# A decoder block with stick-breaking attention: where three parts of its first stage run, and how many buffers its modulation weights have

## The chip, the cores and the metric

The kernel runs on one core of a Trainium2 chip. The core has five engines, each with its own instruction queue: TensorE (matmuls; the profile shows PE, and PEld for its weight loads), VectorE (DVE), ScalarE (ACT), GpSimd (POOL) and SyncE (SP, which here only issues DMAs). Data lies in SBUF (128 partitions), matmul results in PSUM (eight banks of 128 x 512 float32). The metric is the device time of one execution in microseconds (us); lower is better.

## The reference

One layer, batch 1, 1024 tokens, width 1024, all float32. Cut to what matters:

```python
mod = jax.nn.silu(c) @ w_ada + b_ada
shift, scale, gate = jnp.split(mod, 3, axis=-1)
h = rms_norm(x, norm_gain) * (1.0 + scale[:, None, :]) + shift[:, None, :]
proj = h @ w_in                                   # 1024 x 8192
q, k, v, z_a, u, z_b, m_a, m_b = jnp.split(proj, offs, axis=-1)

attn = stick_breaking_attention(q, k, v)          # 16 heads of 64, causal
p_a = (attn * jax.nn.silu(z_a)) @ w_branch_a
pooled = multiscale_causal_pool(u, pool_w, pool_scale)
p_b = (pooled * jax.nn.silu(z_b)) @ w_branch_b
merged = jax.nn.sigmoid(m_a) * p_a + jax.nn.sigmoid(m_b) * p_b
x = x + gate[:, None, :] * (merged @ w_out)
return rms_norm(x, final_gain)
```

The change touches the first three lines and the first columns of `h @ w_in`.

## The kernel before

All large products are done in three matmuls. A float32 operand is split into a high part (a copy rounded to the type `F32R`, the profile's fp32r) and a low part (the operand minus the high part); high x high, high x low and low x high are added up in PSUM. So every weight tile and every block of h costs a copy, mostly on ScalarE, and a subtraction on VectorE or GpSimd.

The stages follow one another: (1) modulation, normalization and transposition of x, h, and the projection to u; (2) the rest of u, then v; (3) pooling, its gate and its branch; (4) attention, between whose steps the matmuls of the other projections are placed; (5) the two output products. The change acts on stage 1, the code under `with pool("init")`, lines 190 to 327. There 1024 is cut into KB = 8 blocks of P = 128.

**The modulation** of block kb needs shift and scale for 128 columns, that is 256 sums over the 1024 elements of silu(c). `load_mod(kb)` (L221) brings the 1 MB weight tile `wa` (128 partitions x 8 x 256) in; the tag "wa" has three buffers, and x4/x5 and x6/x7 later use the same tag. `modulation(kb)` (L227) multiplies the eight slices of 128 x 256 by a scalar per partition (`sc`) and adds them up in `acc` on VectorE: one `tensor_scalar_mul` (L232) and seven `scalar_tensor_tensor` (L234). Two matmuls with a column of ones (L237) then sum over the partitions into the PSUM tile `mps`, which has one bank; two ScalarE instructions make `mod` of it.

**x and h.** `norm_x` (L211) scales a block of 128 tokens: ScalarE sums the squares, GpSimd makes the factor (`st`), VectorE multiplies (L217). `turn_x` (L248) transposes four 128 x 128 blocks on TensorE into the PSUM tile `xt`, of which only one bank is left in this stage. `make_h` (L255) makes the transposed h of a block for 512 tokens: ScalarE applies `mod` (`hf`), ScalarE copies the high part, and the engine that is handed in subtracts for the low part (L260). In the loop over kb it is handed GpSimd (L307), for the second 512 tokens VectorE (L327).

**The first weights.** `first_w(i)` (L265) loads the weight tile of u's column block i (512 KB, two buffers "raw"), copies the high part on ScalarE and subtracts the low part on GpSimd (L271).

**The order.** The loop at L282 runs over kb = 0 to 8. TensorE's instructions, ScalarE's marked ones and the loads of SyncE are pinned to program order (`order`, `load`); VectorE's and GpSimd's instructions are placed by a scheduler at build time, which keeps each queue in a fixed order. A step kb holds a list `todo` of pairs (i, k): column block i of u against block k of h. Column block kb - 1 is new and catches up on all its k, the older ones take k = kb - 1 only; there are six such column blocks (NA) with a PSUM bank each. On TensorE a step is: the high-weight and low-weight matmul of the first pair with the high part of h, the modulation's matmuls, the same two matmuls of the other pairs, one matmul of each pair with the low part of h, and the transposes of block kb + 1. `busy(n)` (L241) adds matmuls whose result is not used, n each at the places that `BUSY` gives; the profile shows them as `ua<-ident,ones` and `ua<-wa,ones`. The SyncE queue takes the loads of wu and wa in turn, and each waits until its buffer is free.

After the loop come column blocks 6 and 7 of u, the second half of x and h, and the next pools.

Of the kernel before, what the change touches and what calls it, by code (L numbers as in the profile page):

```python
# [9 lines left out]
F32 = mybir.dt.float32  # L10
# [5 lines left out]
P = 128  # L16
D = 1024
S = 1024
KB = D // P
# [18 lines left out]
LO_V = (1, 1, 1, 1, 1, 1, 1, 0)  # L38
LO_PB = (1, 1, 1, 1, 1, 1, 2, 2)
HD = 64  # L40
BUSY = (6, 3, 3, 3, 6, 2, 0, 2)
EPS = 1e-6
WINDOWS = (2, 4, 8, 16)
# [5 lines left out]
def block_kernel(ctx, tc, a, out):  # L49
    nc = tc.nc  # L50
    v, act, gp = nc.vector, nc.scalar, nc.gpsimd
# [10 lines left out]
    def bank(tag, name):  # L62
        return psp.tile([P, 512], F32, tag=tag, bufs=BANKS[tag], name=name)
# [3 lines left out]
    g_d = dram.tile([1, D], F32, name="g_d")  # L67
    v_d = dram.tile([NP, P, 8, 4 * HD], F32, name="v_d")
    sb_d = dram.tile([KB, P, S], F32, name="sb_d")
# [6 lines left out]
    ones = const.tile([P, P], F32, name="ones")  # L76
# [11 lines left out]
    def order(op):  # L88
        def issue(*args, **kw):
            ins = op(*args, **kw)  # L90
            if pinned[0]:
                tc.keep_in_program_order(ins)
        return issue

    mm = order(nc.tensor.matmul)
# [94 lines left out]
    with pool("init") as init:  # L190
        sig = const.tile([P, 8], F32, name="csig")
        act.activation(sig, c_v, AF.Sigmoid)
        sc = const.tile([P, 8], F32, name="csilu")
# [8 lines left out]
        def load(dst, src):  # L202
            tc.keep_in_program_order(nc.sync.dma_start(dst, src))

        def load_x(sb):
            if sb in (4, 6):
                pr = init.tile([P, 2, D], F32, tag="wa", bufs=3, name=f"x{sb}")
                xs.extend([pr[:, 0], pr[:, 1]])
            load(xs[sb], a["x"][sb * P:(sb + 1) * P, :])

# [8 lines left out]
        was = {}  # L219

        def load_mod(kb, parts=1):  # L221
            was[kb] = init.tile([P, KB, 2 * P], F32, tag="wa", bufs=3, name=f"wa{kb}")
            n = KB // parts
            for i in range(parts):
                load(was[kb][:, i * n:i * n + n].rearrange("p k c -> p (k c)"), a["w_mod"][kb][:, i * n * 2 * P:(i + 1) * n * 2 * P])

        def modulation(kb):  # L227
            if kb == KB:
                return
            wa = was.pop(kb)  # L230
            acc = init.tile([P, 2 * P], F32, tag="acc", bufs=2, name=f"acc{kb}")
            v.tensor_scalar_mul(acc, wa[:, 0], sc[:, 0:1])  # L232
            for k in range(1, KB):
                v.scalar_tensor_tensor(acc, wa[:, k], sc[:, k:k + 1], acc, ALU.mult, ALU.add)  # L234
            mps = bank("av", f"mps{kb}")
            for i in range(2):
                mm(mps[:, i:i + 1], acc[:, i * P:(i + 1) * P], ones[:, 0:1], start=True, stop=True)  # L237
            order(act.activation)(mod[kb][:, 0:1], mps[:, 0:1], AF.Identity, bias=bada_v[:, kb:kb + 1])
            order(act.activation)(mod[kb][:, 1:2], mps[:, 1:2], AF.Identity, bias=affb[:, kb:kb + 1], scale=gain_v[:, kb:kb + 1])

        def busy(n, mov=ident):  # L241

            for _ in range(n):
                mm(accs[NA - 1][:, :P], ones, mov, start=True, stop=True)
# [3 lines left out]
        def turn_x(sh, kb):  # L248
            pt = xts[sh, kb] = bank("tr", f"xt{sh}_{kb}")
            for i in range(4):  # L250
                transpose(pt[:, i * P:(i + 1) * P], xs[4 * sh + i][:, kb * P:(kb + 1) * P])
                if (sh, kb) == (0, 0) and i < 3:
                    busy(BUSY[1 + i])

        def make_h(sh, kb, lo_eng):  # L255
            hf = init.tile([P, 512], F32, tag="hf", bufs=3, name=f"hf{sh}_{kb}")
            order(act.activation)(hf, xts.pop((sh, kb)), AF.Identity, bias=mod[kb][:, 0:1], scale=mod[kb][:, 1:2])
            sl = slice(sh * 512, sh * 512 + 512)
            order(act.copy)(h_hi[:, kb, sl], hf)
            lo_eng.tensor_sub(h_lo[:, kb, sl], hf, h_hi[:, kb, sl].bitcast(F32))  # L260
# [4 lines left out]
        def first_w(i):  # L265
            raw = wts.tile([P, KB, P], F32, tag="raw", bufs=2, name=f"wu{i}_raw")
            load(raw.rearrange("p k c -> p (k c)"), a["w_in"][CU + i])
            pl, tag, n = (first, "whl0", NA) if i < NA else (wts, "whl", 2)
            hl = pl.tile([P, 2, KB, P], F32R, tag=tag, bufs=n, name=f"wu{i}")
            order(act.copy)(hl[:, 0], raw)  # L270
            gp.tensor_sub(hl[:, 1], raw, hl[:, 0].bitcast(F32))  # L271
            return hl[:, 0], hl[:, 1]

        use = [copy_out(first, 3, u_d[i], f"u{i}") for i in range(KB)]
        load_mod(0, 2)
        for sb in range(4):
            load_x(sb)
            norm_x(sb)
# [3 lines left out]
        for kb in range(KB + 1):  # L282

            kp, sl = kb - 1, slice(0, 512)
            for kind in ("wm" if kb == 0 else "mw"):
                if kind == "m" and kb + 1 < KB:
                    load_mod(kb + 1)
                if kind == "w" and kb < NA:
                    whl.append(first_w(kb))
            todo = [(i, k) for i in range(min(kb, NA)) for k in range(0 if i == kp else kp, kb)]  # L290
            for n, (i, k) in enumerate(todo):
                if n == 1:
                    modulation(kb)
                    if kb == 2:
                        busy(BUSY[6])
                mm(accs[i], whl[i][0][:, k], h_hi[:, k, sl], start=k == 0, stop=False)
                mm(accs[i], whl[i][1][:, k], h_hi[:, k, sl], start=False, stop=False)
            if len(todo) < 2:
                if kb < 2:
                    busy(BUSY[4 * kb], was[0][:, 0, :P] if kb == 0 else ident)  # L300
                modulation(kb)
            for i, k in todo:
                mm(accs[i], whl[i][0][:, k], h_lo[:, k, sl], start=False, stop=k == KB - 1)
            if kb < KB:
                if kb == 0:
                    turn_x(0, 0)
                make_h(0, kb, gp)  # L307
                if kb + 1 < KB:
                    turn_x(0, kb + 1)
                if kb < 2:  # L310
                    busy(BUSY[5 + 2 * kb])
        pinned[0] = False
        for i in range(NA, KB):
            whl.append(first_w(i))
        for sb in range(4, 8):
            load_x(sb)
# [13 lines left out]
    with pool("vp") as vp:  # L330
# [11 lines left out]
        for hf in range(2):  # L342
            if hf == 0:
                wv.append([load_wv(1, k2) for k2 in range(4)])
            for sb in range(8):
                ss = slice(sb * P, (sb + 1) * P)
                ps = bank("pj", f"v{sb}_{hf}")
                for kb in range(KB):
                    hh, hl = h_hi[:, kb, ss], h_lo[:, kb, ss]
# [3 lines left out]

                vo = vp.tile([P, 8, 2, HD], F32R, tag="vo", bufs=3, name=f"vo{sb}_{hf}")
                pv = ps.rearrange("p (h d) -> p h d", d=HD)
                act.copy(vo[:, :, 0], pv)
# [84 lines left out]
    with pool("at") as at:  # L441
# [7 lines left out]
        def pair_tiles(p, use):  # L449

            def tile_(tag, shape, dt=F32R):
                return at.tile([P] + shape, dt, tag=tag, bufs=2, name=f"{tag}_{p}")
# [5 lines left out]
            elif use is use_za:  # L458
                pair[p].update(vv=tile_("vv", [8, 2, 2, HD]), za=tile_("za", [S], F32))

# [224 lines left out]
    with pool("fin") as fin:  # L685
# [29 lines left out]
        for sh in range(2):  # L715
# [24 lines left out]
            for i in range(4):  # L740
                sb = 4 * sh + i
# [86 lines left out]
```

## Time and profile before

| | |
|---|---|
| three runs | 1291.13, 1292.53, 1293.98 us |
| median | 1292.53 us |
| profiled execution | 1294.87 us |
| its span, first to last instruction | 1293.2 us |
| mean granted TensorE clock | 0.990 |
| TensorE busy, whole span | 1241.9 us (96%) |
| VectorE, ScalarE, GpSimd busy | 804.1, 548.1, 279.3 us |
| HBM read and written | 136.86 and 50.34 MB |

How to read the rows. All times are of the one profiled execution, in us unless ns is written. A row of the timeline or of the chain has the start, the duration, the engine, the line of the code, the operation, and the tiles as out<-in; x4 means that four instructions are merged in one row. L90 is the helper `order`, through which all matmuls go, so there the tile tells what it is. A plain float32 matmul leaves two records each for weight load and product. A row of the stretches (A:B) has the stretch's length, then busy time and count of PE, PEld, DVE, ACT and POOL, the granted clock (1.00 is full speed), the mean busy share of the DMA engines, and GB/s. A row by form has the shapes and the count, then total busy time in us and mean ns of one, then the idle time before them and what ended it. A row of waits has the total in us, the number of times and the longest.

### The profile page before, as it was taken

How to read it: one execution, taken by the hardware profiler on the slowest of the kernel's cores; microseconds unless marked ns; L12 is line 12 of the kernel's file. 1: busy time of each engine (PE TensorE's matmuls, PEld its weight loads, DVE VectorE, ACT ScalarE, POOL GpSimd, SP SyncE). 2: the span in 40 equal slices, each digit the busy share in tenths (PEclk: the TensorE clock that was granted, in tenths of full speed). 3: DMA queues.
4: the chain of work that ended last, by engine and by line, in shares of the span. 5: the costliest groups of instructions: out<-in, count | busy, mean ns of one | idle time of the engine just before them, and what ended most of it. 6: DMA issues, size and time to landing. Idle time of an engine off the chain costs nothing.

```text
span 1293.2 us, 16723 instructions
## 1 busy us (share of the span) xinstructions
PE 1241.9 (96%) x6094; PEld 1035.6 (80%) x6094; DVE 804.1 (62%) x1020; ACT 548.1 (42%) x1029; POOL 279.3 (22%) x397
## 2 busy tenths in 40 slices
PE   6799999989999999999999999999999998889997
PEld 5688888768888888888888888888888887667886
DVE  7915342899611177785877768686776743657654
ACT  4445331231101255565656556565655543312101
POOL 4610000102122332322313122231212211400001
PEclk9899999999999999999999999999999999899999
DMA  8528995862343411233323223232322237855512
GB/s 317 204 98 310 330 343 188 303 225 83 113 146 130 155 42 53 70 114 107 122 77 101 80 98 119 90 122 89 99 72 96 96 107 266 288 186 172 183 65 94
DMA packets 72804, 192.48 MB, mean 149 GB/s; under 512 B 7697, under 2 KB 21009, under 8 KB 70802
## 3 DMA queue, kind: packets, MB, share of 16 engines
q1 hardware_dynamic: 63106, 174.38, 39.4%
q10 hardware_dynamic: 9616, 17.04, 3.9%
q8 instruction: 48, 0.79, 0.2%
q14 instruction: 34, 0.28, 0.1%
HBM read 136.86 MB, written 50.34 MB: 145 GB/s over the span
## 4 chain that ended last, share of the span: by engine, by line
PE 78%; DVE 10%; issue 5%; DMA 4%; ACT 1%; POOL 1%; SPq 0%; POOLq 0%; DVEq 0%; ACTq 0%
PE p L90 30%; PE pb L90 7%; PE v L90 7%; PE avs L90 5%; PE o L90 5%; PE wzb L90 5%; PE z L90 5%; PE wt L90 4%; PE u L90 4%; PE pa L90 4%; DVE acc L234 2%; PE ua L90 1%; PE pool L90 1%; DMA wor<-in_w_out 1%; DVE om L557 1%
## 5 line engine op out<-in xcount | busy, mean ns | idle before, releaser
L90 PE MATMUL p<-hT,w 128*128 128x512 f32 x1920 | 538.2, 401 | 0.0
L90 PEld LDWEIGHTS p<-hT,w 128*128 128x128 f32 x1920 | 335.3, 189 | 45.9 <-issue 0.5
L557 DVE TENSOR_TENSOR_SCAN om<-om 128x512 f32<-128x512 f32 (+7 forms) x128 | 175.7, 1372 | 65.7 <-POOL om L555 41.1
L577 DVE TENSOR_TENSOR wt<-wt,wt 128x512 fp32r<-128x512 f32 (+1 forms) x160 | 101.1, 633 | 66.7 <-ACT wt L576 65.4
L550 ACT ACTIVATE om<-z 128x512 f32<-128x512 f32 (+2 forms) x192 | 94.3, 491 | 112.4 <-PE z L90 109.9
L555 POOL TENSOR_SCALAR_AFFINE_SELECT om<-om 128x128 f32<-128x128 f32 x128 | 62.0, 484 | 354.8 <-ACT om L550 318.1
L576 ACT CAST wt<-wt 128x512 fp32r<-128x512 f32 (+1 forms) x160 | 87.2, 545 | 74.9 <-PE wt L90 71.0
L90 PEld LDWEIGHTS avs<-wt,vv 128*128 128x128 f32 x640 | 96.0, 188 | 18.6 <-DVE tp L603 6.7
L558 DVE TENSOR_TENSOR be<-be,om 128x511 f32<-128x511 f32 (+7 forms) x128 | 102.4, 800 | 11.0
L90 PE MATMUL pa<-ga,wa 128*128 128x512 f32 x384 | 94.6, 402 | 10.9 <-DVE ga L698 3.9
L90 PE MATMUL avs<-wt,vv 128*128 128x256 f32 (+1 forms) x640 | 99.8, 278 | 4.5 <-DVE tp L603 4.5
L90 PEld LDWEIGHTS pa<-ga,wa 128*128 128x128 f32 x384 | 73.4, 194 | 31.0 <-DVE ga L698 5.2
L551 ACT ACTIVATE be<-z 128x512 f32<-128x512 f32 (+2 forms) x192 | 93.5, 487 | 0.0
L90 PE MATMUL wzb<-hT,wzb 128*128 128x512 f32 x384 | 92.2, 396 | 0.0
L90 PE MATMUL o<-wo,mhl 128*128 128x512 f32 (+1 forms) x408 | 89.6, 377 | 2.5 <-DVE mhl L114 2.5
L90 PEld LDWEIGHTS wt<-ident,be 128*128 128x128 f32 x576 | 72.4, 141 | 23.6 <-DVE wt L577 1.7
L90 PE MATMUL wt<-ident,be 128*128 128x128 f32 x576 | 89.1, 272 | 0.8 <-DVE wt L577 0.8
L90 PE MATMUL pb<-gb,wb 128*128 128x512 f32 x384 | 88.1, 391 | 0.0
L90 PE MATMUL v<-wv,hT 128*128 128x512 f32 x384 | 87.2, 389 | 0.0
L90 PEld LDWEIGHTS o<-wo,mhl 128*128 128x128 f32 x408 | 73.3, 188 | 17.3 <-DVE mhl L114 3.3
L90 PEld LDWEIGHTS wzb<-hT,wzb 128*128 128x128 f32 x384 | 73.1, 191 | 16.3 <-DVE zs L400 0.3
L90 PEld LDWEIGHTS pb<-gb,wb 128*128 128x128 f32 x384 | 72.1, 188 | 15.8
(118 smaller groups left out, 1538.9 us busy)
## 6 DMA issues: line engine op xcount, KB each, us to landing
w_raw<-in_w_in SPq DMA_DIRECT2D x40, 512.0 KB, 4.4
l_raw<-in_w_in SPq DMA_DIRECT2D x32, 512.0 KB, 5.5
wl_d<-l_raw SPq DMA_DIRECT2D x32, 512.0 KB, 5.0
w<-wl_d SPq DMA_DIRECT2D x32, 512.0 KB, 3.7
v_d<-vo SPq DMA_DIRECT2D x16, 512.0 KB, 5.3
vv<-v_d SPq DMA_DIRECT2D x8, 1024.0 KB, 5.7
wa_raw<-in_w_branch_a SPq DMA_DIRECT2D x16, 512.0 KB, 4.5
wa<-in_w_mod SPq DMA_DIRECT2D x7, 1024.0 KB, 5.5
```

What stands on the lines that cost most here:

```text
L90: ins = op(*args, **kw)
L234: v.scalar_tensor_tensor(acc, wa[:, k], sc[:, k:k + 1], acc, ALU.mult, ALU.add)
L550: act.activation(om[:, b0:b0 + n], zp[:, :n], AF.Sigmoid, scale=-0.125)
L551: act.activation(be[:, b0:b0 + n], zp[:, :n], AF.Sigmoid, scale=0.125)
L555: gp.affine_select(out=tl[:, :P], in_=tl[:, :P], pattern=[[1, P]], compare_op=ALU.is_gt, fill=fill, base=0, channel_multiplier=-1)
L557: v.tensor_tensor_scan(om[:, :W], om[:, :W], om[:, :W], 1.0, ALU.mult, ALU.min)
L558: v.tensor_mul(be[:, 1:W], be[:, 1:W], om[:, :W - 1])
L576: act.copy(wt[:, 0, :off], pt[:, :off])
L577: v.tensor_sub(wt[:, 1, :off], pt[:, :off], wt[:, 0, :off].bitcast(F32))
```

## The change

```diff
+KM = 6
...
         def load_x(sb):
             if sb in (4, 6):
-                pr = init.tile([P, 2, D], F32, tag="wa", bufs=3, name=f"x{sb}")
+                pr = init.tile([P, 2, D], F32, tag="wa", bufs=5, name=f"x{sb}")
...
         def load_mod(kb, parts=1):
-            was[kb] = init.tile([P, KB, 2 * P], F32, tag="wa", bufs=3, name=f"wa{kb}")
+            was[kb] = init.tile([P, KB, 2 * P], F32, tag="wa", bufs=5, name=f"wa{kb}")
...
             v.tensor_scalar_mul(acc, wa[:, 0], sc[:, 0:1])
-            for k in range(1, KB):
+            for k in range(1, KM):
                 v.scalar_tensor_tensor(acc, wa[:, k], sc[:, k:k + 1], acc, ALU.mult, ALU.add)
             mps = bank("av", f"mps{kb}")
             for i in range(2):
-                mm(mps[:, i:i + 1], acc[:, i * P:(i + 1) * P], ones[:, 0:1], start=True, stop=True)
+                for k in range(KM, KB):
+                    mm(mps[:, i:i + 1], wa[:, k, i * P:(i + 1) * P], sc[:, k:k + 1], start=k == KM, stop=False)
+                mm(mps[:, i:i + 1], acc[:, i * P:(i + 1) * P], ones[:, 0:1], start=False, stop=True)
...
             order(act.copy)(hl[:, 0], raw)
-            gp.tensor_sub(hl[:, 1], raw, hl[:, 0].bitcast(F32))
+            v.tensor_sub(hl[:, 1], raw, hl[:, 0].bitcast(F32))
...
                     turn_x(0, 0)
-                make_h(0, kb, gp)
+                make_h(0, kb, v)
```

`acc` now holds the sum of six slices. The other two go through TensorE: wa's slice is the weight, silu(c)'s column the moving operand, and the result is added to the same PSUM column as the sum of acc. For each half i the two new matmuls stand ahead of the one with acc, so with i = 1 they stand behind acc's product for i = 0. The low parts of the first weights (`first_w`, all eight column blocks of u) and of h's first 512 tokens are subtracted on VectorE instead of GpSimd. The tag "wa" has five buffers of 8 KB per partition instead of three.

## The prediction

> **What bounds the kernel now.** First the chain of work that ended last, on the page, then the busy time of the engines in stretches.
>
> ```profile
> span 1293.2 us, 16723 instructions
> ...
> PE 78%; DVE 10%; issue 5%; DMA 4%; ACT 1%; POOL 1%; SPq 0%; POOLq 0%; DVEq 0%; ACTq 0%
> ```
> ```profile
> 0.00:60.42 60.42, 41.80 (x180) 35.32 (x180) 50.56 (x63) 26.36 (x44) 33.59 (x31) 0.92 0.69 261
> 60.42:79.82 19.40, 19.40 (x88) 16.05 (x89) 8.15 (x13) 9.76 (x19) 5.97 (x9) 0.91 0.28 110
> 79.82:224.55 144.73, 144.51 (x650) 119.55 (x649) 52.86 (x54) 55.18 (x73) 5.26 (x18) 1.00 0.77 276
> ```
>
> TensorE carries most of the chain. It is idle 18.6 us (60.42 - 41.80) in the first 60.42 us, and 0.22 us in the 164 us after them. So a change that acts only in the first stage can pay only ahead of 60.42, and what it saves there reaches the end if the later work just starts earlier. The chain in order of time says what holds that stage (start, duration, what):
>
> ```profile
> 42.36 2.46 DVE acc L232
> ...
> 57.90 2.47 DVE acc L234
> ...
> 60.42 0.61 PE mps L90 x4
> 61.02 8.79 PE ua L90 x31
> 69.81 0.44 PE xt L90 x4
> ...
> 70.71 0.34 PE mps L90 x4
> 71.05 3.78 PE ua L90 x16
> ...
> 79.82 10.92 PE u L90 x48
> ```
>
> Up to 60.42 the chain is VectorE's accumulation of the modulation; from there TensorE runs through. The last wait is that for the sum of block 6 (the seventh mps); the eighth, at 70.71, is late for nobody. Some accumulation steps last 2.46 us, others do not. The timeline, with GpSimd's instructions beside VectorE's:
>
> ```profile
> 42.12 2.54 POOL L271 TENSOR_TENSOR wu<-wu_raw,wu 128x1024 fp32r<-128x1024 f32 x1
> ...
> 51.85 8.51 DVE L234 SCALAR_TENSOR_TENSOR acc<-wa,csilu,acc 128x256 f32<-128x256 f32 x7
> ...
> 53.58 1.48 POOL L260 TENSOR_TENSOR hT<-hf,hT 128x512 fp32r<-128x512 f32 x1 [1.92 <-ACT hT L90]
> 55.02 5.06 POOL L271 TENSOR_TENSOR wu<-wu_raw,wu 128x1024 fp32r<-128x1024 f32 x2
> ...
> 60.28 0.34 DVE L232 TENSOR_SCALAR acc<-wa,csilu 128x256 f32<-128x256 f32 x1
> ...
> 60.66 3.61 DVE L234 SCALAR_TENSOR_TENSOR acc<-wa,csilu,acc 128x256 f32<-128x256 f32 x7
> ```
>
> A free step takes 0.34 us (L232) or 3.61/7 = 0.516 us (L234). The long one at 42.36 starts inside GpSimd's subtraction of 42.12 and ends 0.16 us after it; the row of 51.85 takes 8.51 us for seven steps, beside GpSimd rows of 1.48 and 5.06 us. VectorE stands still while GpSimd subtracts. By form, over the first 80 us:
>
> ```profile
> L234 DVE SCALAR_TENSOR_TENSOR acc<-wa,csilu,acc 128x256 f32<-128x256 f32 x56 | 40.4, 726 | 1.8
> L271 POOL TENSOR_TENSOR wu<-wu_raw,wu 128x1024 fp32r<-128x1024 f32 x8 | 20.1, 2518 | 0.0
> L260 POOL TENSOR_TENSOR hT<-hf,hT 128x512 fp32r<-128x512 f32 x8 | 10.9, 1357 | 21.5 <-ACT hT L90 21.5
> L232 DVE TENSOR_SCALAR acc<-wa,csilu 128x256 f32<-128x256 f32 x8 | 9.1, 1137 | 2.9 <-DMA wa<-in_w_mod 2.9
> ```
>
> Against the free steps the stall is 56 x (0.726 - 0.516) + 8 x (1.137 - 0.34) = 18.1 us, nearly all ahead of 60.42.
>
> **The change part by part.** *Two of the eight blocks to TensorE.* VectorE loses 2 x 0.516 = 1.03 us for each of the eight sums; one now costs 0.34 + 5 x 0.516 = 2.92 us. TensorE gains four matmuls for each, of one column with full 128x128 weights. The two matmuls of before appear as four records, so four more are eight records. No such product with wa as weights stands in the trace. Nearest rows: four mps records take 0.34 us on the chain where nothing is waited for (0.085 each); four transposes 0.44 us (0.11); the dearest is a record of 128 columns in the twelve of 21.83 below, 0.21. So eight cost 0.68, 0.88 or 1.65 us. I take 0.88, the transposes', since they too change weights at every record. TensorE takes its work in order: half of them stand ahead of acc's first product, half between its two. Where TensorE waits for acc the first half costs nothing; I count both every time, and put them ahead of the old pair, for in the walk below TensorE is the late one.
>
> *The low parts leave GpSimd.* Eight subtractions of 128x1024 and eight of 128x512 go to VectorE. It does the same forms elsewhere (60 to 230 us):
>
> ```profile
> L105 DVE TENSOR_TENSOR wv<-wv_raw,wv 128x1024 fp32r<-128x1024 f32 x8 | 9.7, 1224 | 6.0 <-ACT wv L110 5.9
> L260 DVE TENSOR_TENSOR hT<-hf,hT 128x512 fp32r<-128x512 f32 x8 | 5.3, 689 | 26.9 <-ACT hT L90 26.9
> ```
>
> 1.22 and 0.69 us, against 2.52 and 1.36 us on GpSimd. VectorE's round per block is then 2.92 + 1.22 + 0.69 = 4.83 us. Before, it was (60.42 - 25.11)/5 = 7.06 us between the waits of blocks 1 and 6, with both mps rows quoted. GpSimd keeps only the tiny st steps, so no long subtraction is left to stall VectorE. A new wait comes with it: the high part is ScalarE's, and behind a waiting subtraction on VectorE's queue stand the next sums. This is the first rival.
>
> *Five buffers instead of three.* What SyncE's queue waited for, and the raw loads' time to land:
>
> ```profile
> SPq L203 <- DVE acc L234: 16.4, 5, 7.4
> ...
> wu_raw<-in_w_in SPq DMA_DIRECT2D x8, 512.0 KB, 5.2
> ```
>
> In the first stage 16.4 us of SyncE's waiting were for sums to free a buffer. But by the chain above no load was late for VectorE, so this earns nothing alone. With quicker rounds it buys distance: a load no longer has to fit between a release and the next sum. The raw loads still wait for their two buffers, in the same queue ahead of later wa loads: 5.2 us to land plus the subtraction, against two rounds of 9.7 us. I cost it at 0, hidden by those two rounds; a load that comes late once costs up to its 5.2 us less the 2.2 us that VectorE is early below, +3.0, and below nothing there is nothing, as no load was on the chain. x4 to x7 are issued after wu7 as before and share these buffers.
>
> *The start.*
>
> ```profile
> 13.39 1.05 ACT L90 CAST wu<-wu_raw 128x1024 fp32r<-128x1024 f32 x1
> 13.45 0.75 DVE L217 TENSOR_SCALAR x<-x,st 128x1024 f32<-128x1024 f32 x1 [0.71 <-POOL st L216]
> 14.85 2.34 POOL L271 TENSOR_TENSOR wu<-wu_raw,wu 128x1024 fp32r<-128x1024 f32 x1
> 14.91 2.83 DVE L217 TENSOR_SCALAR x<-x,st 128x1024 f32<-128x1024 f32 x1 [0.71 <-POOL st L216]
> ...
> 18.37 0.78 ACT L90 ACTIVATE hf<-xt,mod 128x512 f32<-128x512 f32 x1 [3.53 <-PE xt L90]
> ...
> 21.83 2.48 PE L90 MATMUL ua<-ident,ones 128*128 128x128 f32 x12
> ...
> 25.11 0.61 PE L90 MATMUL mps<-ones,acc 128*128 128x1 f32 x4 [0.80 <-DVE acc L234]
> ...
> 27.09 0.62 ACT L90 CAST hT<-hf 128x512 fp32r<-128x512 f32 x1
> 27.12 0.99 PE L90 MATMUL xt<-ident,x 128*128 128x128 f32 x4 [1.07 <-ACT hf L90]
> ```
>
> The scaling of x3 took 2.83 us beside GpSimd's low part of wu0, its neighbour 0.75. Free of it, hf0 starts 2.08 us sooner, at 16.29; if VectorE puts wu0's low part (1.22 us from the cast's end at 13.39 + 1.05 = 14.44) first, 1.33 sooner. I take the middle, 1.7.
>
> *The walk.* The unit for 128x512 is 10.92/48 = 0.23 us. From hf0 to the end of the twelve fillers TensorE needs 21.83 + 2.48 - 18.37 = 5.94 us in a fixed order, so with hf0 at 16.29 they end at 22.23 (the 0.37 us of the middle come off the result). Each step k is then: 0.88 for the new matmuls, 0.34 for the old, 3n - 2 matmuls for the rest of its n pairs, 0.44 for the transposes, 0.46 for the two matmuls of step k + 1. Next h cannot come before 2.60 us after the product of acc begins (27.09 + 0.62 - 25.11), nor the transposes before 2.01 (27.12 - 25.11). The pairs n are 1, 3, 5, 7, 9, 11 for k = 1 to 6, from the loops at L290.
>
> Product of acc 1 begins 22.23 + 0.88 = 23.11; h1 at 25.71, transposes and the two short fillers to 26.4 (0.44 and four records of 0.21 from 25.12). Two matmuls and four new ones: acc 2 at 26.4 + 0.46 + 0.88 = 27.7. h2 at 30.3; acc 3 at 30.3 + 0.46 + 0.88 = 31.7. Its 13 matmuls end at 35.0, past h3 (34.3): from here TensorE alone counts. acc 4 at 35.0 + 0.44 + 0.46 + 0.88 = 36.8; acc 5 at 36.8 + 0.34 + 19 x 0.23 + 1.78 = 43.3; acc 6 at 43.3 + 0.34 + 25 x 0.23 + 1.78 = 51.2. Then 31 matmuls, the transposes, two matmuls and the eighth mps: 51.2 + 0.34 + 7.13 + 0.44 + 0.46 + 1.22 = 60.8, against 71.05 before: 10.3 us sooner. 1.7 us of it are the 31 matmuls, which took 8.79.
>
> VectorE is due before that: from 15.66, wu0's part to 16.9, acc 1 at 19.8, then, with the sums not waiting for anything, rounds of 4.83: 24.6, 29.5, 34.3, 39.1, 44.0, each ahead of TensorE, by 2.2 us at the least. So the bound moves from VectorE to TensorE.
>
> Off that come 0.4 for the start and 0.5 as an allowance for one short wait of VectorE for ScalarE: **9.4 us**. The profiled execution took 1294.87 us (1.67 outside its span); the median shown is 1292.53, 2.34 lower, and I take the gain off the median: 1283.1, given as **1283**. With loads at 0.085 instead of 0.11 it is 7 x 0.2 = 1.4 us lower; at 0.21, 7 x 0.77 = 5.4 higher, 1288.5.
>
> **The clock.** What it was granted in stretches of 2 us (TensorE's busy time, records, clock, DMA) and in one row of the timeline:
>
> ```profile
> 24.00:26.00 2.00, 1.20 (x8) 1.00 0.00 0
> ...
> 28.00:30.00 2.00, 2.00 (x10) 0.50 0.96 399
> ...
> 50.00:52.00 2.00, 2.00 (x14) 1.00 0.00 0
> ```
> ```profile
> 38.55 5.89 PE L90 MATMUL ua<-hT,wu 128*128 128x512 f32 x13
> ```
>
> After waits the clock drops to 0.50 and a matmul costs 5.89/13 = 0.45 us. The row of 28 us follows a stretch (24 to 26) with 1.20 us busy of 2, without one long idle time. The walk has the full clock, because its waits, 1 to 2 us around steps 1 and 2, are shorter and fewer. The Trainium skill (page "TensorE: Matmul & The Clock Gate", section "Part 1: The HAM clock gate") says the array falls to half clock after an idle window of about 3.4 us. By that rule the shorter waits after the change leave the clock full and the third rival has no chance. The fall around 28 us speaks against reading it so strictly, so that rival stays.
>
> **The rivals.** *VectorE's queue becomes one loop with ScalarE* (0.17). If h's low part stands ahead of the next sum, each round is 2.60 + 0.69 + 2.92 = 6.21 us, or 7.43 with wu's part in the loop as well. acc 6 is then at 23.11 + 5 x 7.43 = 60.3 and the eighth mps ends at 69.9: 1.2 us sooner, 1291; with 6.21 and TensorE's step 5 it ends about 64.9, a gain of 6, 1286.5. For it: VectorE goes in order, and the subtraction follows the sum in the code. Against: the sums of later blocks are ready work, and the rows of before show VectorE starting the next block's sum without a pause.
>
> *The gain is given back later* (0.05, 1292). The stretch of 79.82 to 224.55 has a DMA share of 0.77; were it the transfers that set its end, nothing would arrive. Against: TensorE is busy 144.51 of 144.73 us there.
>
> *The clock stays low* (0.07). It is the case that ends on the other side: steps 3 to 6 hold 13 + 21 + 27 + 33 = 94 matmuls, each 0.22 us dearer at half clock. From 9.4/0.22 = 43 of them the gain is gone; at 60 it is 1296, with all 94 about 1304. For it: the rows of 28 and 38 us. Against: from step 3 on the walk has TensorE working without a wait, and the row of 50 us shows 1.00 with TensorE busy throughout.
>
> *It isn't GpSimd that stalls VectorE* (0.03). Then each round gains 1.22 + 0.69 - 1.03 = 0.88 us, and six are 5.3: 1298. Against: the long steps end with GpSimd's subtractions.
>
> *More than the sum* (0.08): loads at 0.085 and waits hidden, 1277 to 1280.
>
> **How the numbers follow.** The forecast, 1280 to 1286, has 0.60. 0.2% of the median is 2.6 us, about what a measurement of this kernel can tell from no change. Faster: 0.60 + 0.08 + 0.12 of the loop rival = 0.80; same: 0.05 of the loop and 0.05 given back = 0.10; slower: 0.07 + 0.03 = 0.10. The range 1279 to 1290 takes in both prices of the weight loads and most of the loop rival; outside are the slower cases and the ends of the others, some 0.2.
>
> **What would show it.** Right: no L232 or L234 step over 0.6 us; mps seven beginning near 51 us, not 60.4; TensorE idle about 10 us ahead of it; the chain of the stage by TensorE from step 3 on. Wrong: mps matmuls over 2 us a block; VectorE idle "until ScalarE's hT" ahead of each sum; clock 0.50 between 32 and 50 us; the matmuls after 79.82 not earlier by the gain.

## The result

| | before | after |
|---|---|---|
| median, nine runs each | 1292.53 us | 1284.49 us |
| lowest to highest | 1291.01 to 1297.50 | 1280.72 to 1289.51 |
| profiled execution | 1294.87 us | 1281.83 us |
| its span | 1293.2 us | 1280.1 us |
| GpSimd busy | 279.3 us | 248.9 us |

The ratio of the times is 0.9935, with a 95% interval of 0.9914 to 0.9957: 8.0 us sooner, 0.6% of the time. The two profiled executions lie 13.0 us apart, more than the medians, since that of before is 2.3 us above its median and that of after 2.7 us below. Timed again in another group, the changed kernel took 1280.31 us (four runs, before 1292.18; ratio 0.9912, 0.9897 to 0.9926), 11.9 us sooner. Nothing below hangs on a single microsecond of a median.

The profile after. The stretches are cut where the same work begins as in those shown of before (columns: length; busy and count of PE, PEld, DVE, ACT, POOL; clock, DMA, GB/s):

```profile
0.00:49.46 49.46, 41.05 (x240) 36.71 (x241) 37.33 (x69) 27.77 (x46) 6.70 (x20) 1.00 0.90 345
49.46:67.48 18.02, 18.02 (x93) 15.22 (x93) 4.34 (x6) 8.94 (x17) 1.73 (x5) 1.00 0.12 47
67.48:212.21 144.73, 144.51 (x649) 119.55 (x649) 52.98 (x54) 55.38 (x73) 5.26 (x18) 1.00 0.79 276
```

What took 60.42 us until the 31 matmuls of step 6 now takes 49.46, TensorE idles 8.4 us there instead of 18.6, and the clock column reads 1.00 instead of 0.92 (how far that column can be trusted is seen under e6). In the last stretch, from the matmuls of u to the end of v, TensorE is busy 144.51 of 144.73 us both times. The chain, in order of time:

```profile
17.55 0.69 DVE hT L264
...
20.39 1.07 PE mps L92 x8
...
28.43 1.23 PE mps L92 x12
29.67 3.10 PE ua L92 x13
32.77 0.44 PE xt L92 x4
33.21 0.47 PE ua L92 x2
33.67 1.23 PE mps L92 x12
...
48.23 1.23 PE mps L92 x12
49.46 7.14 PE ua L92 x31
...
57.51 1.23 PE mps L92 x12
58.74 3.74 PE ua L92 x16
```

Behind the second mps (20.39) the chain crosses ScalarE once, until 22.85 us; from there on it is TensorE without a break, where before VectorE's sums stood. The eighth mps, the last one, ends at 58.74 us instead of 71.05: 12.3 us of the 13.1 us by which the spans differ. This mark is used for all experiments below. From it to the end of the v matmuls the traces of before and after both need 153.5 us (224.55 - 71.05 and 212.21 - 58.74), so what is won ahead of the mark arrives. VectorE's part, by form over 80 us:

```profile
L236 DVE SCALAR_TENSOR_TENSOR acc<-wa,csilu,acc 128x256 f32<-128x256 f32 x40 | 19.2, 483 | 1.0
L275 DVE TENSOR_TENSOR wu<-wu_raw,wu 128x1024 fp32r<-128x1024 f32 x8 | 9.8, 1221 | 1.2 <-ACT wu L92 1.2
L264 DVE TENSOR_TENSOR hT<-hf,hT 128x512 fp32r<-128x512 f32 x10 | 6.9, 690 | 14.1 <-ACT hT L92 14.1
L234 DVE TENSOR_SCALAR acc<-wa,csilu 128x256 f32<-128x256 f32 x8 | 2.8, 350 | 2.8 <-DMA wa<-in_w_mod 2.8
```

No step is stretched any more: 0.483 and 0.350 us instead of 0.726 and 1.137. Between 14 and 60 us the view of waits has only these two rows between TensorE and VectorE's sums, one of the weight loads and one of the products:

```profile
PEld mps L92 <- DVE acc L236: 0.3, 1, 0.3
PE mps L92 <- DVE acc L236: 0.2, 1, 0.2
```

Before, between 14 and 72 us, the products waited 7.5 us:

```profile
PE mps L90 <- DVE acc L234: 7.5, 3, 4.4
```

### The profile page after: what moved, and what is told of

Its sections match the earlier page's. It is cut to its first block, busy times and chain, and to the rows that moved or that the text cites. A ratio compares the mean times of both kernels' runs of the same rounds, so it can differ in the third digit from the quotient of the medians.

```text
span 1280.1 us, 16838 instructions
## 1 busy us (share of the span) xinstructions
PE 1240.3 (97%) x6158; PEld 1036.5 (81%) x6158; DVE 790.0 (62%) x1020; ACT 548.9 (43%) x1029; POOL 248.9 (19%) x381
## 4 chain that ended last, share of the span: by engine, by line
PE 79%; DVE 9%; DMA 5%; issue 5%; ACT 1%; POOL 1%; SPq 0%; POOLq 0%; DVEq 0%; ACTq 0%
PE p L92 30%; PE pb L92 7%; PE v L92 7%; PE avs L92 5%; PE o L92 5%; PE z L92 5%; PE wt L92 4%; PE u L92 4%; PE pa L92 4%; PE ua L92 3%; PE wzb L92 2%; DMA wl_d<-l_raw 1%; DVE om L561 1%; DMA m<-sb_d 1%; DMA l_raw<-in_w_in 1%
```

## The experiments

Each kernel differs from before or after as its diff says (where the buffers of the tag "wa" change, at both of its uses). "The mark" is the end of the eighth mps in its trace.

### The low parts alone (e1), the slices alone (e2), three buffers (e3)

```diff
 e1, against before
-            gp.tensor_sub(hl[:, 1], raw, hl[:, 0].bitcast(F32))
+            v.tensor_sub(hl[:, 1], raw, hl[:, 0].bitcast(F32))
-                make_h(0, kb, gp)
+                make_h(0, kb, v)
 e2, against after
-            v.tensor_sub(hl[:, 1], raw, hl[:, 0].bitcast(F32))
+            gp.tensor_sub(hl[:, 1], raw, hl[:, 0].bitcast(F32))
-                make_h(0, kb, v)
+                make_h(0, kb, gp)
-  tag="wa", bufs=5
+  tag="wa", bufs=3
 e3, against after
-  tag="wa", bufs=5
+  tag="wa", bufs=3
```

> The kernel before with only the low parts (of the first weights and of h) moved to VectorE; all eight slices still summed there, three buffers. The theory (GpSimd's subtractions held VectorE; once they are gone TensorE is the bound): a round on VectorE is 0.34 + 7 x 0.52 + 1.22 + 0.69 = 5.9 us, so the sixth sum is done near 50 us and TensorE, which here has 0.34 us of modulation matmuls a block instead of 1.23, passes the eighth mps at 58 to 61 us: nearly the whole gain, 1283 to 1286. No L234 step is longer than 0.6 us. The rival (the parts add up, and the slices on TensorE bring about half): the eighth mps near 65 us, 1288. The rival that the stalls aren't GpSimd's: long steps stay, and the time is that of before or 5 us more.

> Only the modulation is changed (six slices on VectorE, two on TensorE); the low parts stay on GpSimd, three buffers. The theory: the stalls of some 18 us stay, VectorE stays the bound, and six sums save 6 x 1.03 = 6 us: the eighth mps near 65 us, 1286 to 1288; L234 steps of 1.4 and 2.5 us remain. The rival that the two parts are worth the same each: 1288 and e1 the same. If together e1 and e2 gain more than the whole change, the parts overlap, because the bound has moved to TensorE.

> The changed kernel with three wa buffers again. The theory: the buffers were worth nothing by themselves and little with the quicker rounds: 0 to 3 us above the changed kernel, SyncE waits for sums again. The rival: with rounds of 5 us a load of 5 us that starts only at a release is late for every sum, VectorE waits for wa, and 5 us or more are lost.

| | time, us | ratio to before (95%) | mark, us |
|---|---|---|---|
| e1 | 1286.47 | 0.9956 (0.9939 to 0.9973) | 61.43 |
| e2 | 1289.21 | 0.9975 (0.9960 to 0.9989) | 70.66 |
| e3 | 1282.23 | 0.9918 (0.9903 to 0.9934) | 58.85 |

e3 is as after: the two more buffers bring nothing that shows here. The groups by form of e1 (first row) and of e2 (the other three) show what makes VectorE's steps long:

```profile
L234 DVE SCALAR_TENSOR_TENSOR acc<-wa,csilu,acc 128x256 f32<-128x256 f32 x56 | 25.1, 482 | 0.5
```
```profile
L236 DVE SCALAR_TENSOR_TENSOR acc<-wa,csilu,acc 128x256 f32<-128x256 f32 x40 | 32.9, 824 | 1.4
L275 POOL TENSOR_TENSOR wu<-wu_raw,wu 128x1024 fp32r<-128x1024 f32 x8 | 20.3, 2534 | 1.0 <-ACT wu L92 1.0
L264 POOL TENSOR_TENSOR hT<-hf,hT 128x512 fp32r<-128x512 f32 x8 | 11.1, 1382 | 20.5 <-ACT hT L92 20.5
```

Once GpSimd subtracts nothing, 56 steps take 0.482 us each although all eight slices are still summed; with six slices and GpSimd at work they take 0.824. In e1's chain VectorE is the bound up to 33.73 us and TensorE from there:

```profile
33.28 0.41 DVE acc L234
...
33.73 0.61 PE mps L90 x4
34.33 4.68 PE ua L90 x13
39.01 0.44 PE xt L90 x4
39.44 0.46 PE ua L90 x2
39.91 0.34 PE mps L90 x4
```

So the first steps are where fewer slices on VectorE can still help. e1 and e2 were each slower than expected. In e1 the 13 matmuls of step 3, right behind a wait of 2.93 us for VectorE, took 4.68 us instead of the 3.10 of after; the clock was at 0.50 from 34.66 to 38.05 us. The trace of e2 is of the slowest of its ten executions (1294.35 us, 5.1 above their median), so it doesn't explain the median, and its mark is not typical. What it shows of that execution: from 28 to 44 us the clock was at half speed, and TensorE, not VectorE, held the stage (VectorE waited 7.8 us in all for the mps matmuls, which read acc and so free one of its two buffers):

```profile
28.00:32.00 4.00, 4.00 (x18) 3.81 (x17) 3.93 (x3) 0.76 (x3) 3.35 (x2) 0.50 0.67 274
...
40.00:44.00 4.00, 4.00 (x10) 3.08 (x10) 2.71 (x4) 1.90 (x3) 2.95 (x2) 0.50 0.90 359
```
```profile
DVE acc L234 <- PE mps L92: 7.8, 3, 4.0
```

Whether the parts overlap, the times don't tell: 6.1 us (e1) and 3.3 us (e2) make 9.4 us together, the change 8.0 or 11.9. The low parts alone are the larger part, and move the mark by 9.6 of the 12.3 us.

### GpSimd's work back without its use (e5)

One more subtraction on GpSimd for each first weight, whose result is not read, and four wa buffers instead of five (e3 shows that even three cost nothing):

```diff
             v.tensor_sub(hl[:, 1], raw, hl[:, 0].bitcast(F32))
+            scr = init.tile([P, KB, P], F32, tag="scr", bufs=1, name=f"scr{i}")
+            gp.tensor_sub(scr, hl[:, 0].bitcast(F32), hl[:, 0].bitcast(F32))
```

> The changed kernel with four wa buffers and, for each first weight, one more subtraction of 128x1024 on GpSimd whose result nobody reads: only GpSimd's use of the memory comes back, no dependence. The theory (GpSimd's reading and writing stalls VectorE by itself): each of the eight takes 2.5 us and stretches one VectorE instruction by about 2 us, L236's mean goes from 0.48 to about 0.8 us, VectorE's round from 4.8 to 6.9 us, and the eighth mps ends 3 to 6 us later: 1286 to 1290. The rival (the long steps came from the waits of the dependent work, not from GpSimd being busy): no long step, and the time of the changed kernel.

Measured: 1290.78 us, ratio 0.9988 (0.9974 to 1.0002), mark at 68.94 us. That is 10.2 us later than after, where 3 to 6 were expected. Eight instructions of which nothing depends take back nearly the whole gain. Groups by form:

```profile
L236 DVE SCALAR_TENSOR_TENSOR acc<-wa,csilu,acc 128x256 f32<-128x256 f32 x40 | 28.7, 718 | 1.0
L277 POOL TENSOR_TENSOR scr<-wu 128x1024 f32<-128x1024 f32 x8 | 16.2, 2019 | 26.8 <-ACT wu L92 26.8
```

L236 went from 0.483 to 0.718 us as expected (40 x 0.235 = 9.4 us). In the chain VectorE's steps of 2.0 to 2.1 us are back, and a late one hands the delay on: wu's low part on VectorE frees the raw buffer late, the next load starts late, and step 6 waits for it. Behind that wait its 31 matmuls take 8.75 us instead of 7.14. These two links are what the expectation left out.

```profile
45.16 2.01 DVE acc L236
...
49.19 1.15 DVE wu L275
50.36 4.09 DMA wu_raw<-in_w_in
54.48 1.04 ACT wu L92
...
56.82 1.23 PE mps L92 x12
58.05 8.75 PE ua L92 x31
```

This shows the cause that the prediction only inferred from rows that coincide. The Trainium skill (page "SBUF — State Buffer", section "Who interferes with whom") says that the two engines share a pair of ports under an exclusive lock, and that a VectorE instruction with two inputs in SBUF contends there with a GpSimd instruction that reads SBUF. The steps of L236, which read wa and acc, agree: 2.01 us against 0.48, beside GpSimd subtractions of 2.02 us.

### Which low parts (e10, e11)

e10 is after with h's low parts on GpSimd (`make_h(0, kb, gp)`), e11 after with the first weights' low parts there (`gp.tensor_sub` in `first_w`).

> The changed kernel, but h's low parts stay on GpSimd; only those of the first weights are on VectorE. The theory (VectorE only has to keep ahead of TensorE): GpSimd's eight shorter subtractions stall VectorE by 0.9 us each, a round on VectorE is 2.9 + 1.2 + 0.9 = 5.0 us, still quicker than TensorE's steps 4 to 6 of 5 to 8 us: within 1 us of the changed kernel, 1280 to 1283. The rival (every stall counts): 8 x 0.9 - 8 x 0.7 and the longer 1.36 us of GpSimd on h's way, 3 us or more later, 1284 to 1287.

> The changed kernel, but the first weights' low parts stay on GpSimd; only h's are on VectorE. The theory: the long subtractions stall VectorE by 2.1 us each, a round is 2.9 + 0.7 + 2.1 = 5.7 us, and the start is late again by 1 to 2 us as x3's scaling is stretched: the eighth mps at 62 to 66 us, 1285 to 1289. The rival (the two low parts are worth the same, or only the number of VectorE's instructions counts): as e10.

Measured: e10 1283.39 us, 0.9928 (0.9912 to 0.9945), mark 62.18; e11 1287.55 us, 0.9958 (0.9943 to 0.9973), mark 65.10. The long subtractions matter more, as expected. For e10 the theory missed: its mark is 3.4 us behind that of after, where it had 1 us at most and its rival 3 or more. The chain shows where:

```profile
20.75 1.07 PE mps L92 x8
...
25.10 2.42 PE mps L92 x12
...
31.85 1.23 PE mps L92 x12
...
37.11 1.23 PE mps L92 x12
```
```profile
20.00:24.00 4.00, 2.32 (x18) 1.93 (x18) 3.82 (x8) 2.81 (x6) 0.12 (x1) 1.00 1.01 416
24.00:28.00 4.00, 4.00 (x19) 3.71 (x19) 3.86 (x8) 1.21 (x3) 1.31 (x1) 0.53 0.89 311
28.00:32.00 4.00, 4.00 (x17) 3.23 (x15) 3.89 (x6) 2.40 (x4) 1.29 (x1) 0.61 0.76 288
```

It is level with after at the second mps (20.75 and 20.39), 3.4 us behind at the fourth (31.85 and 28.43), and not further behind at the fifth (37.11 and 33.67). Between them the clock was at about half. From step 3 on VectorE's slack hides GpSimd's stalls, as the theory had it, and the rival's way (every stall counts) is not what cost the time. Before that, TensorE had waited 0.61 us for the second sum, against 0.23 in after; then the clock fell, at about 24.3 us, and the 3rd to the 4th mps took 6.75 us instead of 4.02. That the longer wait brought on the fall is argued from this order, not tried.

### Fillers and clock (e6, and the changed kernel again)

e6 is after with `BUSY = (0,) * 8`, no filler matmuls.

> The changed kernel without any filler matmul. The theory (TensorE bounds the stage, and its clock depends on how busy it was): the clock is at 0.50 through steps 1 to 4, some 45 matmuls cost 0.22 us more, less 2 us of fillers saved: 4 to 8 us later, 1288 to 1292. The rival (the fillers only stand in the way once VectorE is quick): 1 to 2 us sooner.

> The changed kernel itself once more, as the base of this group and for a second profile of it. Expected 1280 to 1286. In the first profile TensorE's records ran at full speed from 14.6 us on, and the eighth mps ended at 58.74 us. If that early start was a matter of the clock's phase in that execution, it comes later here (records of 128 columns at 0.21 us until some 25 us) and the eighth mps 2 to 3 us later; if it belongs to the kernel, it is the same to 0.3 us.

e6: 1288.07 us, 0.9975 (0.9962 to 0.9987), mark 63.92: 5.2 us later at the mark, within what was expected. The fillers, useless as results, are worth their time. The changed kernel again has its mark at 58.61 us, the same to 0.13, with the same early start, so the start is no accident of one execution; its time is given above. How TensorE's speed is read here, for e6 first:

```profile
28.00:32.00 4.00, 4.00 (x13) 3.22 (x14) 3.89 (x9) 2.85 (x5) 0.00 (x0) 1.00 0.89 315
```
```profile
31.36 1.05 PE L92 MATMUL xt<-ident,x 128*128 128x128 f32 x4
37.78 0.60 PE L92 MATMUL xt<-ident,x 128*128 128x128 f32 x4
```
```profile
22.85 0.66 PE L92 MATMUL xt<-ident,x 128*128 128x128 f32 x4 [1.07 <-ACT hf L92]
```

Four transposes take 1.05 us at 31 us in e6 and 0.60 at 38; in after 0.66 at 23 already. Yet the clock column of e6 says 1.00 at 28 to 32 us. Ahead of its first change the column can't be trusted; the durations can. So after, too, ran at half speed until 14.8 us: six fillers took 1.49 us at 13.02 and 0.97 at 14.51.

### Slices back to VectorE where TensorE is the bound (e4, e7, e8)

```diff
-KM = 6
+KM = (6, 6, 6, 6, 8, 8, 8, 8)
...
-            for k in range(1, KM):
+            for k in range(1, KM[kb]):
...
-  mm(mps[:, i:i + 1], acc[:, i * P:(i + 1) * P], ones[:, 0:1], start=False, stop=True)
+  mm(mps[:, i:i + 1], acc[:, i * P:(i + 1) * P], ones[:, 0:1], start=KM[kb] == KB, stop=True)
 e7, on top of e4
-BUSY = (6, 3, 3, 3, 6, 2, 0, 2)
+BUSY = (14, 3, 3, 3, 6, 2, 0, 2)
-                    busy(BUSY[4 * kb], was[0][:, 0, :P] if kb == 0 else ident)
+                    busy(BUSY[4 * kb])
 e8, on top of e7
-BUSY = (14, 3, 3, 3, 6, 2, 0, 2)
+BUSY = (24, 5, 5, 5, 6, 2, 0, 2)
                 make_h(0, kb, v)
+                if kb < 2:
+                    busy(4)
```

> The changed kernel, but blocks 4 to 7 are summed wholly on VectorE again (six slices for blocks 0 to 3). The theory: from step 3 on TensorE is the bound and VectorE has slack, so the 0.89 us of each new group of matmuls is lost time there: 3 to 3.6 us sooner than the changed kernel at the eighth mps (about 55.5 us), near 1281. The rival (VectorE still bounds the late steps): no gain, or up to 4 us lost, as each sum costs 1.03 us more.

> The kernel with blocks 4 to 7 summed wholly on VectorE, once more, for a second profile and a firmer time. In its first profile the early records ran at half speed until some 20 us, in both of the changed kernel's only until 14.5 us. If that is the phase of the clock in one execution, it can be early here, and the eighth mps then ends near 55.5 us; if it belongs to the kernel, it is late again, at 58.2 us. Time 1278 to 1281.5.

> The kernel with blocks 4 to 7 summed wholly on VectorE, and the first fillers run on the identity from the start of the kernel, 14 instead of 6, without waiting for the first weights. The theory: TensorE is then busy from about 2 us, its clock is full by 10 us in every execution, and the first steps run at full speed: the eighth mps near 55.5 us instead of 58.3, 1278 to 1280, with less spread between executions. The rival (the clock rises at 14 or at 26 us whatever was done before): 1281 as without.

> As e4, with fillers meant to leave TensorE no gap before step 2: 24 on the identity from the start instead of 6 that wait for weights, 5 instead of 3 between the first transposes, and 4 more ahead of the transposes of steps 0 and 1. The theory: with no gap the clock rises before 10 us and stays at full speed, so the first steps lose nothing: the eighth mps near 55.5 us, 1277 to 1279.5. The rival (fillers in these places only stand in the way, the clock falls by other gaps): 58 us or later, 1281 or more.

| | time, us | ratio to before (95%) | mark, us |
|---|---|---|---|
| e4 | 1281.16 | 0.9913 (0.9898 to 0.9927) | 58.25 |
| e4 again | 1281.48 | 0.9912 (0.9897 to 0.9928) | 57.96 |
| e7 | 1280.10 | 0.9909 (0.9895 to 0.9924) | 59.67 |
| e8 | 1279.57 | 0.9899 (0.9883 to 0.9914) | 57.39 |

e4's chain, to be held against those of after and e1 above:

```profile
32.76 3.07 PE ua L92 x13
...
36.72 0.34 PE mps L92 x4
...
57.91 0.34 PE mps L92 x4
```

From the start of the fifth mps to the mark after needs 58.74 - 33.67 = 25.07 us, e4 58.25 - 36.72 = 21.53: the four late groups of new matmuls cost 3.5 us, as expected. But e4 came to the fifth mps 3.05 us later than after. Its early matmuls ran slower, in both its profiles (one row of each kernel):

```profile
19.98 1.87 PE L92 MATMUL ua<-ident,ones 128*128 128x128 f32 x12
24.49 1.12 PE L92 MATMUL xt<-ident,x 128*128 128x128 f32 x4 [1.06 <-ACT hf L92]
```
```profile
18.32 1.50 PE L92 MATMUL ua<-ident,ones 128*128 128x128 f32 x12
```

Against e1, whose start was as slow, e4 is at the fifth mps 39.91 - 36.72 = 3.2 us sooner, and from there both take 21.5 us. So the slices on TensorE bring 3.2 us in the first blocks, where VectorE is the bound, and give back 3.5 us in the last four, where TensorE is. Half of the 3.2 comes through the clock: without its wait for VectorE, e4 does the 13 matmuls of step 3 in 3.07 us, e1 in 4.68. By these traces the slices are worth about nothing to the change as a whole; that the mark of after lies 2.7 us ahead of e1's goes with its early full speed, which is not shown to come from the slices.

e7 and e8 missed the 55.5 us of their expectation. e7 was at full speed from 5 us, but fell back twice: from 11.9 to 15.3 us, after its fillers had ended ahead of the first mps and TensorE had waited there (0.32, 1.13 and 1.43 us), and from 22.1 to 32.3 us, so that the third mps takes 2.35 us. e8 closes most of those gaps. It ran at full speed from the first transposes on, and then VectorE, with eight slices in the late blocks, was late there twice, by 0.84 us (34.60) and 0.71 us (41.30); the third wait in this row is the 0.23 us at the second mps that after has too:

```profile
PE mps L92 <- DVE acc L236: 1.8, 3, 0.8
```

e8 has the lowest time of all, but its interval and that of the changed kernel's second timing overlap, so that it beats the change is not shown. Neither is a gain of e4 over the change.

## Why the prediction was right

*The bound.* Right. VectorE's sums, stretched by GpSimd, held the stage up to 60.42 us; e1 and e5 take the stretch away and bring it back with nothing else in common. In after the longest L236 step is 0.486 us, and the seventh mps begins at 48.23 us.

*The price on TensorE.* Right: a group of mps matmuls takes 1.23 us against 1.22 in the sum.

*The walk.* The step that was mis-sized is the start, "from hf0 to the end of the twelve fillers". The sum took 5.94 us for it, measured 18.32 + 1.50 - 16.09 = 3.73. The rows of before from which it came had run at half speed (twelve fillers in 2.48 us, 1.50 in after), which the clock column (1.00) did not show. hf0 itself began 2.28 us sooner than before (16.09), a little more than the 2.08 of the estimate. From the second mps on the sum fits: from its end (23.45 in the sum, 21.46 measured) to the mark 37.35 us were forecast and 37.28 measured. So the mark came at 58.74 instead of 60.8. Where the start is slow, as in e4, this pessimism is right.

*The allowance for VectorE waiting for ScalarE.* It shrank to one place: h0's low part stood inside the second sum (17.55 in the chain), and TensorE waited 0.23 us. Elsewhere the scheduler put sums ahead, and the loop rival did not come about: from 14 to 60 us VectorE never waited for h's high part, and once, 1.2 us, for a weight's.

*Nothing for the buffers.* Right: e3.

*Given back later.* No: 153.5 us from the mark to the end of v in both traces.

*The clock.* In the profiled execution of after it stayed full from 14.8 us to the end of the stage. As a mechanism this rival was real: e10 lost 2.7 us to it between two steps, e2 ran at half speed from 27 to 44 us and e6 up to 34. Short waits were enough in e10, where TensorE's longest idle time ahead of the fall was 1.07 us; so it was right to keep this rival although the waits are short. The nine timed runs of after point the same way: their mean granted clock was 0.993 to 0.996 in the three fastest and 0.988 in the two slowest. Where in the kernel the slower ones lost it is not traced.

*The total.* 1283 was forecast, 1284.49 and 1280.31 were measured. That the first is so close is in part luck: at the mark the profiled execution gained 12.3 us where 9.4 were forecast, and the median of the nine, at a lower clock (0.990 against 0.994), gave 2.7 us of it back.

What stays open: why after (twice), e3 and e10 reached full speed by 15 us and before, e1, e2, e4 (twice), e5 and e11 only after 16 us or later, although e4 asks the same of TensorE up to there. The clock's own records in the traces narrow it down. Their changes lie whole multiples of 3.41 us apart (in before at 23.88, 27.30, 30.71, 37.54, 44.36 and 61.43 us), so here the clock changes only on a fixed raster, and where the raster lies against the work differs from trace to trace. In the nine traces with the work of after on TensorE up to there, the four early ones have a mark of the raster between 0.62 us ahead of the first transpose's start and 0.28 us behind it, the five late ones between 0.79 and 1.35 us ahead. That is read off, not tried, and why two traces of one kernel agree so well stays open too.

## What to carry to other kernels

A helper engine is not free because it has time: eight subtractions on GpSimd, whose results nobody waited for, cost some 10 us through the engine beside it and what waited for that one (e5), so look for instructions of one form with two durations and see what ran beside the long ones. Work moved to another engine pays only in the steps where that engine waits; here the same move gained 3.2 us in the first four blocks and lost 3.5 us in the last four. When a term of the sum is taken from rows, make sure at which clock they ran, by the duration of an instruction that is known elsewhere.

## What the runs showed of the hardware

In these traces the clock column reads 1.00 until the first recorded change, also while matmuls take twice their time: e6 has 1.00 at 28 to 32 us and 1.05 us for four transposes that take 0.60 us later. The clock also falls without a long idle time: in e10 TensorE was busy 2.32 of the 4 us from 20 to 24, with no idle time over 1.07 us, and 4.00 of the next 4, which were granted 0.53. In after it was busy 2.70 of the same 4 us and kept its clock. In e8, with fillers from 1.57 us on and 3.46 of those 4 us busy, the records of 128 columns took 0.13 us from 11.4 us on, and no half-speed stretch came before 240 us.
